# Moving matmul operands to chosen byte offsets within a partition: three unused tiles in a two-layer decoder trunk

## The chip, the cores and the metric

The kernel runs on one core of one Trainium2 chip. The metric is the device time of one execution in microseconds, as the median of several runs. Loading the inputs from the host is not in it; every weight is read from the chip's HBM within it.

## The reference

Two decoder layers over 256 tokens with a model width of 1024, in float32. Layer 0 mixes tokens with multi-head latent attention, layer 1 with MoBA block attention (at 256 tokens it is one causal block) and a shared relative bias. A dense MLP follows each.

```python
def sq_relu_mlp(h, w_in, w_out):          # (256,1024) @ (1024,4096), then @ (4096,1024)
    a = jax.nn.relu(h @ w_in)
    return (a * a) @ w_out

for i in range(2):
    h = rms_norm(x, attn_norm[i])
    x = x + (mla_mixer(h, ...) if i == 0 else moba_mixer(h, ...))
    h = rms_norm(x, mlp_norm[i])
    x = x + sq_relu_mlp(h, mlp_w_in[i], mlp_w_out[i])
```

## The kernel before

All activations are held transposed, the feature dimension over the 128 partitions. For precision, each operand of a large matmul is split into a high part (`fp32r`, a rounded float32) and a low part, the rest. One product is then three matmuls into the same PSUM tile: high by high, low weight by high, high weight by low. `mm3` issues them, and `mm` (L77) is the line of nearly every matmul.

The weights stream through `units`, each a 128 by 1024 tile (4096 bytes in a partition) or less. SP loads a unit into one of four `raw` tiles, ScalarE rounds it into a `wh` tile (`hi`, L141), VectorE subtracts to make `wl` (`lo`, L150). `wh` and `wl` are rings of seven tiles each. The helper `fill` puts these conversions between groups of matmuls; the order of all instructions is written out by hand.

What the matmuls read:

- `hT` is the pair `hTh`, `hTl`, the normalized input of a layer, 8 blocks of 256 columns (1024 bytes each). The first half of an MLP (`first`) streams a block of it against 128 columns of a weight unit: 8 blocks by 3 matmuls make 24 for one output of 256 columns, 16 such outputs for each of two rounds `r`.
- `a` is the pair of hidden activations of an MLP, 16 blocks of 256 columns, and lives in the MLP's own pool. The second half of a round streams its 16 blocks against weight columns: 48 matmuls for each of 8 outputs `d`, so 384 in a round.
- `aT` is the pair of attention outputs, 8 blocks of 256 columns, one per head, in the pool of a layer's heads. The output projection (`o` and `col` in `run_heads`) streams it: 24 matmuls for each of 8 outputs.
- In the projections of queries, keys and values the roles are exchanged: the weights stream (512 columns), and `hT`, `cqT` or `ckvT` is the stationary operand.

In these, each column block of a weight unit is 512 bytes and each block of an activation 1024, so all slices of one tile start at the same remainder to 512. The pools lie one after the other in each partition, in the order in which they are opened: `const`, `wraw`, `wsp`, `work`, `small`, then the pools of the layers. From the sizes of the tiles, the starts before are:

| tile | start, bytes | past a multiple of 512 |
|---|---|---|
| `hTh`, `hTl` (in `const`) | 30848, 39040 | 128 |
| `raw`, `wh`, `wl` (4096 bytes each) | from 47264, 63648, 92320 | 160 |
| `aT`, layer 0 | 211168, 219360 | 224 |
| `aT`, layer 1 | 202240, 210432 | 0 |
| `a`, both MLPs | 178688, 195072 | 0 |
| `cqT`, `ckvT` | 164576 and on | 224 |

Of the kernel before, what the change touches and what calls it, by code (L numbers as in the profile page):

```python
# [10 lines left out]
F32 = mybir.dt.float32  # L11
# [5 lines left out]
AX = mybir.AxisListType  # L17

P = 128
D = 1024  # L20
S = 256
NT = S // P
KD = D // P
H = 8
# [16 lines left out]

GAINS = [("attn0", KD), ("attn1", KD), ("mlp0", KD), ("mlp1", KD), ("qa", QR // P), ("kva", KVR // P),
         ("qn", 1), ("kn", 1), ("mq", 1), ("mk", 1), ("thr", 1)]
# [6 lines left out]
NR = 2  # L50
NPAIR = DFF // (2 * P * NR)
RAW = 4
# [4 lines left out]
def trunk(ctx: ExitStack, tc: tile.TileContext, A, out):  # L57
    nc = tc.nc
    ctx.enter_context(tc.manual_schedule())
    const = ctx.enter_context(tc.tile_pool(name="const", bufs=1))  # L60
# [5 lines left out]

    def ps():
        return psum.tile([P, 512], F32, name="ps", tag="ps")

    def t2(*shape):  # L70
        return work.tile([P, *shape], F32, name="t2", tag="t2")

    def f32(ap):
        return ap.bitcast(F32)

    def mm(o, a, b, start, stop):
        nc.tensor.matmul(o, a, b, start=start, stop=stop)  # L77

    def mm3(o, a, b, start, stop):

        mm(o, a[0], b[0], start, False)
        mm(o, a[1], b[0], False, False)
        mm(o, a[0], b[1], False, stop)
# [69 lines left out]
    def fill(n=1):  # L153
        lo(n)
        hi(n)

    def unit(i):
        while len(his) <= i:
            hi()
        while len(los) <= i:  # L160
            lo()
        return his[i], los[i]

    def done(i):

        used[0] = max(used[0], i + 1)

    def part(u, sl):
        return u[0][:, sl], u[1][:, sl]
# [9 lines left out]
    rowc = const.tile([P, HALF + 2 * PE_D], F32)  # L179
    xs = early.tile([P, NT, D], F32)  # L180
    warm = const.tile([P, 1], F32)
# [4 lines left out]
    nc.scalar.activation(warm, warm, AF.Sin)  # L186

    pz = ps()
    for _ in range(8):
        mm(pz, zeros[:, :P], zeros, True, True)  # L190
# [49 lines left out]

    hTh = const.tile([P, KD, S], F32R)
    hTl = const.tile([P, KD, S], F32R)

    def make_h(k, gname):

        nc.scalar.activation(hTh[:, k], x[:, k], AF.Copy, scale=gain(gname, k))
        nc.vector.scalar_tensor_tensor(hTl[:, k], x[:, k], gain(gname, k), f32(hTh[:, k]),
                                       op0=OP.mult, op1=OP.subtract)

    def hT(k, sl=slice(None)):  # L250
        return hTh[:, k, sl], hTl[:, k, sl]
# [33 lines left out]
    def row_scale(name, ss):  # L285

        m = small.tile([P, NT], F32, name="me_" + name, bufs=1)
        nc.vector.tensor_scalar(m, ss, 1.0 / D, EPS, op0=OP.mult, op1=OP.add)
        r = small.tile([P, NT], F32, name="rs_" + name, bufs=1)
# [44 lines left out]
    def to_T(y, dst, g):  # L334

        pt = ps()
        yf = y.rearrange("p a b -> p (a b)")
        for i in range(4):
            nc.tensor.transpose(pt[:, i * P:(i + 1) * P], yf[:, i * P:(i + 1) * P], ident)  # L339
        src = pt.rearrange("p (a b) -> p a b", b=P)  # L340
        if g is None:
            nc.scalar.copy(dst, src)
        else:
            nc.scalar.activation(dst, src, AF.Copy, scale=g)
# [52 lines left out]
    for k in range(KD):  # L397
# [6 lines left out]
        lo()  # L404
    LK = KVR + PE_D
    latq = [ps()[:, :QR] for _ in range(NT)]
    latk = [ps()[:, :LK] for _ in range(NT)]

# [37 lines left out]
    ssl = small.tile([P, 4, NT], F32, name="ssl", bufs=1)  # L446
    sqj = [early.tile([P, D], F32, name=f"sqj{i}") for i in range(2)]

# [36 lines left out]
    def head_tiles(l):  # L485

        cm = ExitStack()
        pool = cm.enter_context(tc.tile_pool(name=f"heads{l}", bufs=1))
        r = []
        for c in range(2):  # L490
            r.append({n: pool.tile([P, *sh], F32, name=f"{n}{c}")
                      for n, sh in (("k", (HG, S)), ("q", (HG, S)), ("v", (NT, HG, P)))})
        aT = [pool.tile([P, H, S], F32R, name=f"aT{i}") for i in range(2)]
        return cm, r, aT

# [260 lines left out]
    def mean_squares(i, n):  # L756
        nc.vector.scalar_tensor_tensor(msl[:, i], ssl[:, 1 + i], 1.0 / n, me0, op0=OP.mult, op1=OP.add)
        nc.vector.tensor_scalar(epsm[:, i], msl[:, i], EPS, None, op0=OP.mult)

    nc.vector.tensor_scalar(me0, ssl[:, 0], EPS / D, EPS * EPS, op0=OP.mult, op1=OP.add)  # L760
    mean_squares(0, KVR)
# [8 lines left out]
    lo()  # L770
    early_ctx.close()
    heads_ctx, hd, aT = head_tiles(0)
    mean_squares(2, QR)

# [14 lines left out]
    for o, a, b in rope_halves(m[:, :, 0], m[:, :, 1]):  # L789
        a, b = (i[:, :, None, :].to_broadcast([P, NT, 2, HALF]) for i in (a, b))  # L790
# [45 lines left out]
    def mlp(l, base, fillers, finish):  # L836

        with tc.tile_pool(name=f"mlp{l}", bufs=1) as pool:
            scale = pool.tile([P, S], F32, name="scale")
            a = [pool.tile([P, 2 * NPAIR, S], F32R, name=f"a{i}") for i in range(2)]  # L840
            sums = SumSquares()

            def first(b, r, j, split_k):
                u = [unit(b + 2 * j + i) for i in range(2)]
                if split_k:
                    o = [ps()[:, :S] for _ in range(2)]
                else:
                    p = ps()
                    o = [p[:, f * S:(f + 1) * S] for f in range(2)]
                for f, k in [(f, k) for k in range(KD) for f in range(2)] if split_k else \  # L850
                        [(f, k) for f in range(2) for k in range(KD)]:
                    c = (k % 4) * 256 + f * P
                    mm3(o[f], part(u[k // 4], slice(c, c + P)), hT(k), k == 0, k == KD - 1)
                fill(2)
                for g in fillers:
                    if g[0] == (r, j):
                        g[1]()
                for f, n in ((0, 1), (1, 1)) if split_k else ((0, 2),):
                    src = o[f] if split_k else p
                    rl = t2(n * S)  # L860
                    nc.scalar.activation(rl, src, AF.Relu)  # L861
                    sq = t2(n * S)
                    nc.vector.scalar_tensor_tensor(sq, src, 0.0, rl, op0=OP.max, op1=OP.mult)  # L863
                    ah, al = (i[:, 2 * j + f:2 * j + f + n].rearrange("p a b -> p (a b)") for i in a)
                    nc.scalar.copy(ah, sq)  # L865
                    nc.vector.tensor_sub(al, sq, f32(ah))  # L866
                done(b + 2 * j + 1)

            for r in range(NR):
                b = base + r * (2 * NPAIR + 2 * KD)  # L870
                for j in range(NPAIR):
                    first(b, r, j, r == 0 and j == 0)
                    if r == 0 and 1 <= j < 5:
                        sums.add(j - 1)
                    if r == 0 and j == 5:
                        s = sums.total()
                    if r == 0 and j == 6:
                        pb = ps()
                        mm(pb[:, :S], ones, s, True, True)
                        nc.vector.tensor_scalar(scale, pb[:, :S], 1.0 / D, EPS, op0=OP.mult, op1=OP.add)  # L880
                        nc.vector.reciprocal(scale, scale)
                b += 2 * NPAIR
                for d in range(KD):
                    o = ps()[:, :S]
                    for f in range(2 * NPAIR):
                        u = unit(b + 2 * d + f // 8)
                        c = (f % 8) * P
                        mm3(o, part(u, slice(c, c + P)), (a[0][:, f], a[1][:, f]), f == 0, f == 2 * NPAIR - 1)
                        if f == 7:
                            fill()  # L890
                            done(b + 2 * d)
                    fill()
                    for g in fillers:
                        if g[0] == (r, NPAIR + d):
                            g[1]()
                    y = t2(S)
                    nc.vector.tensor_tensor(y, o, scale, op=OP.mult)  # L897
                    if r < NR - 1:
                        nc.gpsimd.tensor_add(x[:, d], y, x[:, d])  # L899
                    else:  # L900
                        finish(d, y)
                    done(b + 2 * d + 1)
# [70 lines left out]


    heads_ctx, hd1, aT1 = head_tiles(1)
    order1 = {"k0": 0, "q0": 1, "v0": 2, "k1": 3, "v1": 4, "q1": 5}
    r3, sq3 = [None], [None]
# [138 lines left out]
```

## Time and profile before

| | us |
|---|---|
| median of 3 runs | 584.32 (583.97 to 585.66) |
| the profiled execution, whole time | 585.61 |
| its span, first to last instruction | 583.8 |
| TensorE (PE) busy | 572.6 |
| PE weight loads (PEld) busy | 546.3 |
| VectorE (DVE) busy | 406.8 |
| ScalarE (ACT) busy | 307.0 |
| GpSimd (POOL) busy | 114.0 |

Matmuls are pipelined: the duration of one is longer than the distance from its start to the next one's start. Where the text speaks of a pitch, it is that distance, the mean of many.

### The profile page before, as it was taken

The numbers are of one execution on the slowest core, as the hardware profiler recorded it, in microseconds if no ns is written. First come the engines' busy times: TensorE is split into PE (matmuls) and PEld (weight loads), VectorE is DVE, ScalarE is ACT, GpSimd is POOL, SyncE is SP. The second block draws the span as 40 slices with busy tenths as digits, with TensorE's granted clock in tenths as the row PEclk, the third lists the DMA queues.
The fourth block names the chain that finished last, engine by engine and source line by source line (L and its number), as shares of the span: only waits on it lengthen the run. The fifth ranks groups of instructions, "written<-read, shape, count | busy, mean of one in ns | idle before, by whom it ended". The sixth has DMA issues, their size and how long they took to land.

```text
span 583.8 us, 10767 instructions
## 1 busy us (share of the span) xinstructions
PE 572.6 (98%) x4346; PEld 546.3 (94%) x4346; DVE 406.8 (70%) x646; ACT 307.0 (53%) x492; POOL 114.0 (20%) x119
## 2 busy tenths in 40 slices
PE   8898999999999999999999999999999999999997
PEld 6877999999999999999988888999999999999997
DVE  5697877678899987786648456776778555666541
ACT  5688775665523355544545465756664333555420
POOL 5875100022132200024314100000231322000100
PEclk9899999999999999999999999999999999999999
DMA  7732535565645546475644554345466665465630
GB/s 285 280 92 73 182 111 161 174 189 173 216 146 170 184 154 217 161 234 184 209 152 134 194 177 138 116 145 180 144 186 207 186 185 179 151 207 173 225 120 28
DMA packets 29265, 99.54 MB, mean 171 GB/s; under 512 B 4032, under 2 KB 4672, under 8 KB 29216
## 3 DMA queue, kind: packets, MB, share of 16 engines
q1 hardware_dynamic: 28736, 97.92, 52.6%
q0 software_dynamic: 336, 0.92, 0.4%
q8 instruction: 34, 0.56, 0.4%
q14 instruction: 15, 0.12, 0.1%
q10 hardware_dynamic: 144, 0.02, 0.0%
HBM read 97.79 MB, written 1.05 MB: 169 GB/s over the span
## 4 chain that ended last, share of the span: by engine, by line
PE 92%; POOL 4%; DMA 1%; DVE 1%; issue 1%; ACT 1%; SPq 0%; POOLq 0%
PE ps L77 90%; POOL hrs L238 1%; PE ps L339 1%; PE ps L535 1%; DMA rowc<-in_rowc 1%; POOL pr L370 1%; POOL rr L371 1%; POOL t L730 0%; POOL kk L365 0%; POOL kk L364 0%; DVE cqT L461 0%; DVE wl L150 0%; POOL scl L238 0%; ACT wh L141 0%; POOL t L779 0%
## 5 line engine op out<-in xcount | busy, mean ns | idle before, releaser
L141 ACT CAST wh<-raw 128x1024 fp32r<-128x1024 f32 x177 | 183.1, 1046 | 111.7 <-DMA raw<-in_w_out_mlp 63.2
L150 DVE TENSOR_TENSOR wl<-raw,wh 128x1024 fp32r<-128x1024 f32 x177 | 228.1, 1319 | 8.5 <-ACT wh L141 8.2
L77 PE MATMUL ps<-a,wh 128*128 128x256 f32 x1024 | 186.8, 283 | 0.0
L77 PEld LDWEIGHTS ps<-a,wh 128*128 128x128 f32 x1024 | 158.2, 188 | 0.0
L77 PE MATMUL ps<-hTh,wh 128*128 128x256 f32 x512 | 144.6, 282 | 0.0
L77 PE MATMUL ps<-a,wl 128*128 128x256 f32 x512 | 143.8, 281 | 0.0
L77 PE MATMUL ps<-hTh,wl 128*128 128x256 f32 x512 | 143.8, 281 | 0.0
L77 PE MATMUL ps<-hTl,wh 128*128 128x256 f32 x512 | 143.8, 281 | 0.0
L77 PEld LDWEIGHTS ps<-a,wl 128*128 128x128 f32 x512 | 97.0, 190 | 0.0
L77 PEld LDWEIGHTS ps<-hTh,wl 128*128 128x128 f32 x512 | 96.5, 188 | 0.1
L77 PEld LDWEIGHTS ps<-hTh,wh 128*128 128x128 f32 x512 | 96.5, 188 | 0.1
L77 PEld LDWEIGHTS ps<-hTl,wh 128*128 128x128 f32 x512 | 96.5, 188 | 0.0
L77 PE MATMUL ps<-aT,wh 128*128 128x256 f32 x256 | 51.3, 290 | 0.0
L77 PE MATMUL ps<-wh,hTh 128*128 128x512 f32 (+2 forms) x128 | 47.0, 397 | 1.6 <-ACT wh L141 1.5
L77 PE MATMUL ps<-wh,hTl 128*128 128x512 f32 (+2 forms) x128 | 45.3, 382 | 0.0
L899 POOL TENSOR_TENSOR x<-t,x 128x256 f32<-128x256 f32 x16 | 26.4, 1650 | 96.2 <-DVE t L897 96.2
L77 PE MATMUL ps<-wl,hTh 128*128 128x512 f32 (+2 forms) x128 | 45.0, 380 | 0.0
L863 DVE SCALAR_TENSOR_TENSOR t<-ps,t 128x512 f32<-128x512 f32 (+1 forms) x34 | 22.4, 658 | 28.9 <-ACT t L861 28.9
L897 DVE TENSOR_TENSOR t<-ps,scale 128x256 f32<-128x256 f32 x32 | 13.5, 421 | 40.7 <-PE ps L77 40.7
L77 PEld LDWEIGHTS ps<-aT,wh 128*128 128x128 f32 x256 | 40.6, 188 | 0.2
L866 DVE TENSOR_TENSOR a<-t,a 128x512 fp32r<-128x512 f32 (+1 forms) x34 | 22.5, 662 | 22.5 <-ACT a L865 22.5
L238 POOL TENSOR_TENSOR hrs<-hss,mhalf 128x4 f32<-128x4 f32 (+1 forms) x18 | 25.0, 1400 | 64.1 <-DVE hss L314 48.8
(157 smaller groups left out, 650.5 us busy)
## 6 DMA issues: line engine op xcount, KB each, us to landing
raw<-in_w_in_mlp SPq DMA_DIRECT2D x64, 512.0 KB, 4.1
raw<-in_w_out_mlp SPq DMA_DIRECT2D x64, 512.0 KB, 4.3
raw<-in_w_qkv SPq DMA_DIRECT2D x24, 512.0 KB, 4.0
raw<-in_w_u SPq DMA_DIRECT2D x8, 512.0 KB, 6.1
win<-in_w_in SPq DMA_DIRECT2D x8, 352.0 KB, 5.6
raw<-in_w_o0a SPq DMA_DIRECT2D x4, 512.0 KB, 3.5
raw<-in_w_o0b SPq DMA_DIRECT2D x4, 512.0 KB, 3.5
raw<-in_w_o1a SPq DMA_DIRECT2D x4, 512.0 KB, 4.2
```

The source lines that it names most:

```text
L77: nc.tensor.matmul(o, a, b, start=start, stop=stop)
L141: (eng.copy if eng is nc.scalar else eng.tensor_copy)(his[i][:, :w], raws[i][:, :w])
L150: eng.tensor_sub(los[i][:, :w], raws[i][:, :w], f32(his[i][:, :w]))
L238: nc.gpsimd.tensor_tensor(dst, t, mhalf[:, :n].rearrange("p (a b) -> p a b", b=t.shape[-1]) if len(t.shape) == 3 else mhalf[:, :n], op=OP.pow)
L339: nc.tensor.transpose(pt[:, i * P:(i + 1) * P], yf[:, i * P:(i + 1) * P], ident)
L370: eng.tensor_scalar(pr, kk, c, None, op0=OP.mult)
L371: eng.tensor_sub(rr, src, pr)
L535: nc.tensor.transpose(pt[:, i * P:(i + 1) * P], self.p[:, i * P:(i + 1) * P], ident)
L863: nc.vector.scalar_tensor_tensor(sq, src, 0.0, rl, op0=OP.max, op1=OP.mult)
L866: nc.vector.tensor_sub(al, sq, f32(ah))
L897: nc.vector.tensor_tensor(y, o, scale, op=OP.mult)
L899: nc.gpsimd.tensor_add(x[:, d], y, x[:, d])
```

## The change

A helper `room` allocates a tile that no instruction reads or writes. It is called three times: 416 bytes in `const` behind `hTh` and `hTl`, 224 bytes in the MLP's pool ahead of `a`, and 224 bytes in the heads' pool of layer 1 ahead of `aT` (0, so none, in layer 0). No instruction is added, removed or moved; what follows a room in a partition starts later.

```diff
+ROOM = {"hT": 416, "aT0": 0, "aT1": 224, "a": 224}
...
+    def room(pool, name):
+        if ROOM[name]:
+            pool.tile([P, ROOM[name] // 4], F32, name="room_" + name)
...
     hTh = const.tile([P, KD, S], F32R)
     hTl = const.tile([P, KD, S], F32R)
+    room(const, "hT")
...
+        room(pool, f"aT{l}")
         aT = [pool.tile([P, H, S], F32R, name=f"aT{i}") for i in range(2)]
...
             scale = pool.tile([P, S], F32, name="scale")
+            room(pool, "a")
             a = [pool.tile([P, 2 * NPAIR, S], F32R, name=f"a{i}") for i in range(2)]
```

The starts past a multiple of 512 after it, by the same sums: `hT` 128 (unmoved), `raw`, `wh` and `wl` 160 + 416 = 576, so 64; `aT` of layer 0 224 + 416 = 640, so 128; `aT` of layer 1 and `a` 0 + 416 + 224 = 640, so 128; `cqT` and `ckvT` 128.

## Rows read from the trace of the kernel before

**Rows 1.** The page: busy time of each engine; granted clock in 40 slices.

```profile
PE 572.6 (98%) x4346; PEld 546.3 (94%) x4346; DVE 406.8 (70%) x646; ACT 307.0 (53%) x492; POOL 114.0 (20%) x119
...
PEclk9899999999999999999999999999999999999999
```

**Rows 2.** The page: the chain that ended last, by engine.

```profile
PE 92%; POOL 4%; DMA 1%; DVE 1%; issue 1%; ACT 1%; SPq 0%; POOLq 0%
```

**Rows 3.** Groups by shape, PE: xcount | busy us, mean ns | idle before.

```profile
L77 PE MATMUL ps<-a,wh 128*128 128x256 f32 x1024 | 186.8, 283 | 0.0
L77 PE MATMUL ps<-hTh,wh 128*128 128x256 f32 x512 | 144.6, 282 | 0.0
L77 PE MATMUL ps<-a,wl 128*128 128x256 f32 x512 | 143.8, 281 | 0.0
L77 PE MATMUL ps<-hTh,wl 128*128 128x256 f32 x512 | 143.8, 281 | 0.0
L77 PE MATMUL ps<-hTl,wh 128*128 128x256 f32 x512 | 143.8, 281 | 0.0
L77 PE MATMUL ps<-aT,wh 128*128 128x256 f32 x256 | 51.3, 290 | 0.0
L77 PE MATMUL ps<-wh,hTh 128*128 128x512 f32 x96 | 38.7, 403 | 0.0
...
L77 PE MATMUL ps<-aT,wl 128*128 128x256 f32 x128 | 35.8, 280 | 0.0
```

**Rows 4.** Timeline of PE, second MLP: start us, duration us, operation, xcount merged.

```profile
441.88 0.28 PE L77 MATMUL ps<-a,wh 128*128 128x256 f32 x1
...
487.95 0.28 PE L77 MATMUL ps<-hTh,wh 128*128 128x256 f32 x1
...
533.38 0.28 PE L77 MATMUL ps<-a,wh 128*128 128x256 f32 x1
```

**Rows 5.** Timeline of PE, output projection of layer 0: first and last.

```profile
87.70 0.28 PE L77 MATMUL ps<-aT,wl 128*128 128x256 f32 x1
...
100.19 0.28 PE L77 MATMUL ps<-aT,wh 128*128 128x256 f32 x1
```

**Rows 6.** Timeline of PE, output projection of layer 1: first and last.

```profile
383.17 0.28 PE L77 MATMUL ps<-aT,wl 128*128 128x256 f32 x1
...
395.89 0.28 PE L77 MATMUL ps<-aT,wh 128*128 128x256 f32 x1
```

**Rows 7.** Timeline of PE, projections of layer 1: first and last.

```profile
288.73 0.39 PE L77 MATMUL ps<-wh,hTh 128*128 128x512 f32 x1
...
305.29 0.39 PE L77 MATMUL ps<-wl,hTh 128*128 128x512 f32 x1
```

**Rows 8.** Timeline of PE, a query projection of layer 0: first and last.

```profile
33.02 1.56 PE L77 MATMUL ps<-wh,cqT 128*128 128x512 f32 x6
...
38.62 0.86 PE L77 MATMUL ps<-wl,cqT 128*128 128x512 f32 x3
```

**Rows 9.** Timeline of PE, two heads of layer 1, operands in full float32.

```profile
356.60 0.81 PE L77 MATMUL ps<-pT,v 128*128 128x256 f32 x4
357.25 0.82 PE L77 MATMUL ps<-k,q 128*128 128x128 f32 x4
```

**Rows 10.** Windows: us, busy (xcount) by engine, granted clock, DMA share, GB/s.

```profile
160.00:170.00 10.00, 10.00 (x90) 9.93 (x88) 9.76 (x14) 3.67 (x4) 3.31 (x2) 1.00 0.46 128
...
441.00:488.00 47.00, 47.00 (x394) 47.00 (x393) 28.21 (x27) 18.49 (x20) 11.53 (x7) 1.00 0.65 192
488.00:533.00 45.00, 45.00 (x382) 45.00 (x382) 28.83 (x31) 24.35 (x30) 1.65 (x1) 1.00 0.53 175
```

**Rows 11.** Waits from 396 us on: waiter <- releaser: us in total, times, longest.

```profile
ACT wh L141 <- DMA raw<-in_w_out_mlp: 36.9, 29, 3.6
```

## The prediction

> **What bounds the kernel now.** I read the page from the top. TensorE is busy for 98% of the span at nearly the full granted clock [rows 1], and the chain of work that ended last runs through it for 92% [rows 2]. The groups by shape show which matmuls these are: 1536 that stream `hT` (three groups of 512), 1536 that stream `a` (1024 and 512) and 384 that stream `aT` (256 and 128), all of 256 columns and with 0.0 us idle before them [rows 3]. The reader is to see that nothing ahead of TensorE holds it up in these groups; in the windows of the second MLP it is busy for 47.00 of 47 us and 45.00 of 45, at a granted clock of 1.00 [rows 10]. There the time is the number of matmuls times their pitch, and the only thing that the change can touch on this path is the pitch.
>
> The duration column is no pitch (283 ns for one matmul, while the next starts sooner), so I took pitches from the timeline, and found that they differ by tile although all are 128 by 256 with the same kind of weights:
>
> - `hT`: from 487.95 to 533.38 us stand one round's 16 outputs of 24, so 384 matmuls: 45.43 / 384 = 118.31 ns [rows 4].
> - `a`: from 441.88 to 487.95 us, 8 outputs of 48, again 384: 46.07 / 384 = 119.97 ns [rows 4].
> - `aT` in layer 0: 107 matmuls from 87.70 to 100.19 us: 12.49 / 106 = 117.83 ns [rows 5].
> - `aT` in layer 1: 107 matmuls from 383.17 to 395.89 us: 12.72 / 106 = 120.00 ns [rows 6].
>
> The last two are the telling pair. They come from the same lines of code in the same order, and one has the pitch of `a`, the other does not. What `aT` of layer 1 has in common with `a` is its start, 0 past a multiple of 512; `aT` of layer 0 starts at 224. The weights start at 160 in all four. So the pitch goes with where the operands start, by about 2 ns of 120, and the sum is made of such differences.
>
> **The change part by part.** It issues nothing, so there is no instruction to cost. It moves three things on the path: the weights from 160 to 64, `a` and `aT` of layer 1 from 0 to 128, `aT` of layer 0 from 224 to 128. `hT` stays at 128. In each large matmul of 256 columns the streamed tile then starts 64 bytes past the weights in the 512-byte grid.
>
> Before, only `aT` of layer 0 stands so (224 - 160 = 64), and it has the lowest pitch. `hT` is at 128 - 160 = -32 and `a` at -160. I take the distance between the two operands as what decides, so 117.83 ns for all, since it is the one row that shares something with every pair after the change. The terms:
>
> - `a`: 1536 x (119.97 - 117.83) = 3.29 us [rows 3 to 5].
> - `hT`: 1536 x (118.31 - 117.83) = 0.74 us [rows 3 to 5].
> - `aT` of layer 1: 192 x (120.00 - 117.83) = 0.42 us [rows 5, 6].
> - `aT` of layer 0: the distance stays, 0.
>
> That is 4.45 us. But the exact pair (128 with 64) is in no row, and the weights at a multiple of 64 are in none, so the price of a matmul is bounded from both sides. Below, by the wide matmuls: with `hT` stationary, 72 of 512 columns take 288.73 to 305.29 us, 16.56 / 71 = 233.24 ns, half of which is 116.62 ns for 256 columns [rows 7]. A matmul of twice the columns for each weight load has less room for a meeting of the two reads, so I take that as the pitch with none. Above, by the dearest row, 119.97. I choose 117.83 between them because the same distance gave it.
>
> The wide matmuls themselves have the weights as the streamed operand: distance 160 - 128 = 32 before, 64 - 128 = -64 after. With `cqT` stationary (start 224) it is -64 already before, and 24 of them from 33.02 to 38.62 us take 5.60 / 24 = 233.3 ns [rows 8], the same as at 32. So their term is 0.
>
> The engines that convert weights and activations get new addresses too; I cost that at nothing. In the second MLP VectorE is busy for 28.21 of 47 us and ScalarE for 18.49 [rows 10], and cover remains if their operations get a tenth longer. The tightest place is in the first MLP, where the bias blocks are made: VectorE is busy for 9.76 us of a window of 10 [rows 10]. If TensorE gets 1.8% faster there, VectorE needs 9.94 of 10. It still fits; if it did not, at most the gain of that half round is lost, 384 x 2.14 ns = 0.8 us. DMA moves at a share of 0.65 in the busier window [rows 10]; ScalarE waits for its loads, 36.9 us in the last third [rows 11], but its results are early, as TensorE shows no idle time there. A 2% faster consumer leaves that so.
>
> **Sum.** The profiled execution took 585.61 us, 1.81 us more than its span of 583.8, and stands 1.29 us above the median of 584.32. The saving lies inside the span, so I subtract it from the median: 584.32 - 4.45 = 579.9 us.
>
> **A rule that speaks against it.** By rows 5 and 6 the start of an operand goes with the pitch. The Trainium skill (SBUF — State Buffer, section "Who interferes with whom") gives TensorE two independent SBUF read ports, one for the moving operand and one for weight loads, and says that it never waits on anyone. By that rule the starts could not matter and the time would stay at 584.3 us. The rows show 117.83 against 120.00 ns, so I side with them, but keep the rule's outcome as a rival.
>
> **The rivals.**
>
> *The streamed tile's own start decides, not the distance.* `hT` lies at 128 already and shows 118.31 ns; after the change all of them lie there. Then `a` saves 1536 x 1.66 = 2.55 us, `aT` of layer 1 192 x 1.69 = 0.32, `aT` of layer 0 loses 192 x 0.48 = 0.09: 584.32 - 2.78 = 581.5 us. For it: `a` and `aT` of layer 1 share start and pitch. Against: the same two share the distance as well, so the rows can't tell.
>
> *No meeting is left.* All four go to 116.62 ns: 1536 x 1.69 + 1536 x 3.35 + 192 x 3.38 + 192 x 1.21 = 8.6 us, so 575.7. For it: the starts become multiples of 64 on both sides, which no pair before has. Against: nothing in the rows shows that this helps.
>
> *The base rate was held up too.* The full float32 matmuls run 768 columns (two heads, 256 + 128 each) in 0.65 us [rows 9], 0.846 ns a column. If the split ones could run at half of that, 0.423, 256 columns would take 108.3 ns; so 1536 x 10.0 + 1536 x 11.7 + 192 x 11.7 + 192 x 9.5 = 37.4 us, and with 288 wide ones (three groups of 96 [rows 3]) at 216.6, 288 x 16.6 = 4.8 us more: 542 us. Against: the wide matmuls show 0.456 ns a column at two different distances [rows 7, 8], so this base has not moved with the start.
>
> *Nothing changes.* The difference between the two `aT` comes from something else that differs between the layers, and the room does no more than shift addresses: 584.3. Against: the pitch of `a` repeats in `aT` of layer 1 within 0.03 ns.
>
> *Slower: weights at 64 meet the streamed tile worse.* The two tiles whose streamed start is a multiple of 64 (`hT`, `a`) have the higher pitches, the one whose start is not (`aT` of layer 0) the lowest. After the change all are multiples of 64, and the weights too. If that puts every pair at the level of `a`, `hT` loses 1536 x 1.66 = 2.55 us and `aT` of layer 0 192 x 2.14 = 0.41: 587.3 us. It decides from a mean pitch of about 119.1 ns on, the mean of `hT` and `a` now.
>
> **How the numbers follow.** The distance decides: 0.36 (579.9 us, its own range 578.5 to 581.2). The streamed start decides: 0.18. No meeting left: 0.20. Base rate: 0.04. Nothing: 0.10. Slower: 0.12. A measurement of this kernel can't tell less than about 0.3%, 1.75 us, from no change. The gains by distance, by start and by the lowest pitch lie beyond that; with a little of the second falling short, faster has 0.76, the same 0.12, slower 0.12. The range leaves out the base rate and the slower case (0.16): from 575.7 to 584.3, with the runs' own scatter of 0.9 us on both sides, 574.8 to 585.2.
>
> **What the profile after would show.** If the forecast holds: one round of `a` in the second MLP takes 384 x 117.8 = 45.2 us instead of 46.07, one of `hT` 45.2 instead of 45.43, `aT` of layer 1 falls to that of layer 0, and wide matmuls stay at 233 ns. If the streamed start decides, `a` falls to 118.3 and `hT` keeps its pitch, while `aT` of layer 0 rises. TensorE stays busy throughout and its granted clock at 1.00. The prediction is wrong if `hT`, whose tile does not move, changes by more than 1 ns, for then the weights' own start counts for more than the distance; or if gaps appear between the outputs in the first MLP, where VectorE has little room.

## The result

The changed kernel took 581.18 us (median of 6 runs, 580.05 to 581.82) against 584.15 for the kernel before (6 runs, 583.66 to 585.66): a ratio of 0.9938, 95% interval 0.9923 to 0.9952. The forecast was 579.9 us with a range of 574.8 to 585.2. Timed again on another occasion against 11 runs of before, it came out at 0.9911 (0.9896 to 0.9926). The forecast saving of 4.45 us, a ratio of 0.9924, lies at the edge of both intervals, which is where the first part of the execution comes in (below).

The page of the changed kernel, busy time and granted clock, answers to [rows 1]:

```profile
span 579.5 us, 10767 instructions
PE 567.9 (98%) x4346; PEld 541.0 (93%) x4346; DVE 406.6 (70%) x646; ACT 307.0 (53%) x492; POOL 115.8 (20%) x119
...
PEclk9998999999999999999999999999999999999999
```

The instructions are the same in number. TensorE's busy time fell by 4.7 us, that of its weight loads by 5.3 and the span by 4.3; POOL's rose by 1.8, and those of DVE and ACT hardly moved. The timeline of PE in the second MLP, at the same places as [rows 4]:

```profile
439.47 0.28 PE L84 MATMUL ps<-a,wh 128*128 128x256 f32 x1
...
484.70 0.28 PE L84 MATMUL ps<-hTh,wh 128*128 128x256 f32 x1
...
529.93 0.28 PE L84 MATMUL ps<-a,wh 128*128 128x256 f32 x1
```

Both rounds of 384 now take 45.23 us, 117.79 ns a matmul, where `a` took 46.07 and `hT` 45.43. The output projections of layer 0 and of layer 1, the first and the last of 107 matmuls each, answer to [rows 5, 6]:

```profile
87.68 0.28 PE L84 MATMUL ps<-aT,wl 128*128 128x256 f32 x1
...
100.16 0.28 PE L84 MATMUL ps<-aT,wh 128*128 128x256 f32 x1
...
381.21 0.28 PE L84 MATMUL ps<-aT,wl 128*128 128x256 f32 x1
...
393.70 0.28 PE L84 MATMUL ps<-aT,wh 128*128 128x256 f32 x1
```

12.48 / 106 = 117.7 ns and 12.49 / 106 = 117.8: layer 1 has come down from 120.0 to the pitch that layer 0 had all along. The wide matmuls, 72 from 286.74 to 303.30 us, take 16.56 / 71 = 233.2 ns, as in [rows 7].

**Where the saving sits.** The first matmul of the first MLP, in the timelines of before and after:

```profile
100.31 0.28 PE L77 MATMUL ps<-hTh,wh 128*128 128x256 f32 x1
...
100.28 0.28 PE L84 MATMUL ps<-hTh,wh 128*128 128x256 f32 x1
```

It starts at 100.31 us before and at 100.28 after, so nothing was gained ahead of it. From there to the end of the span it is 583.8 - 100.31 = 483.5 us before and 579.5 - 100.28 = 479.2 after: all of the 4.3 us. By stretches, 1.96 us of it lie between the start of the first MLP and the wide matmuls (188.42 to 186.46 us), 0.23 in the output projection of layer 1 (13.03 to 12.80) and 2.12 in the second MLP (183.34 to 181.22, first start to last).

**Why the medians differ less.** Windows of the changed kernel (us, busy and count by engine, granted clock, DMA share, GB/s):

```profile
30.00:45.00 15.00, 13.15 (x60) 9.88 (x59) 14.60 (x30) 11.77 (x34) 13.12 (x12) 1.00 0.31 89
45.00:50.00 5.00, 4.70 (x22) 3.78 (x21) 3.41 (x6) 2.92 (x12) 3.99 (x4) 0.66 0.30 108
```

The same kernel in another profiled execution:

```profile
10.00:15.00 5.00, 3.97 (x15) 3.97 (x16) 4.47 (x8) 4.54 (x9) 4.41 (x8) 0.66 1.04 405
...
45.00:50.00 5.00, 4.70 (x32) 3.88 (x31) 3.46 (x7) 4.29 (x17) 3.99 (x4) 1.00 0.34 108
```

In the first, the granted clock falls to its lower level (1.2 instead of 2.4 GHz) for part of the window from 45 to 50 us, after 15 us in which TensorE was busy for 13.15. In the second it falls earlier, between 10 and 15 us, and not again after 15 us with the same busy time; ten more matmuls fit into the last window, and the first MLP starts at 98.76 us instead of 100.28. The early fall was made up at once: from 20 to 25 us TensorE is busy for 4.43 us in the second execution and for 2.88 in the first. The profile of before has its fall between 20 and 30 us (0.83). So where the clock falls moved the start of the first MLP by some 1.5 us between two executions of one kernel. Behind it the second profile needs 577.9 - 98.76 = 479.1 us, like the first. It was the median of before that differed between the two occasions (584.15 and 585.51 us; the changed kernel had 581.18 and 581.16). A scatter of 1.5 us is large enough for that, but of before only one execution has a trace, so it is not shown that the clock was the cause there.

### The profile page after: what moved, and what is told of

Its sections match the earlier page's. It is cut to its first block, busy times and chain, and to the rows that moved or that the text cites. A ratio compares the mean times of both kernels' runs of the same rounds, so it can differ in the third digit from the quotient of the medians.

```text
span 579.5 us, 10767 instructions
## 1 busy us (share of the span) xinstructions
PE 567.9 (98%) x4346; PEld 541.0 (93%) x4346; DVE 406.6 (70%) x646; ACT 307.0 (53%) x492; POOL 115.8 (20%) x119
## 4 chain that ended last, share of the span: by engine, by line
PE 92%; POOL 4%; DVE 1%; DMA 1%; issue 1%; SPq 0%; ACT 0%; POOLq 0%
PE ps L84 90%; POOL hrs L245 1%; PE ps L347 1%; PE ps L544 1%; DMA rowc<-in_rowc 1%; POOL pr L378 1%; POOL rr L379 1%; POOL t L739 0%; POOL kk L373 0%; POOL kk L372 0%; DVE sqj L462 0%; DVE cqT L469 0%; DVE wl L157 0%; POOL scl L245 0%; POOL rr L383 0%
## 5 line engine op out<-in xcount | busy, mean ns | idle before, releaser
L84 PE MATMUL ps<-a,wh 128*128 128x256 f32 x1024 | 183.5, 280 | 0.0
L84 PEld LDWEIGHTS ps<-a,wl 128*128 128x128 f32 x512 | 95.8, 187 | 0.0
```

## The experiments

All but the first have the change's `room` helper and one more call ahead of `hTh`, so that any start can be set; the edits are given against the changed kernel. "Distance" is the start of the streamed tile less that of the weights. Pitches are worked out from the timeline, over a round of 384 matmuls of the second MLP for `hT` and `a`, over 106 intervals for `aT`. Experiments 3 to 7, 9 and 10 are one execution each (584.75, 583.47, 585.68, 581.14, 584.77, 574.07 and 580.69 us), so their pitches and stretches are read and not their times.

**1. The changed kernel once more** (no edit).

> The changed kernel itself, unchanged, timed in five rounds. Its traced span fell by 4.3 us against that of before (583.8 to 579.5), while the medians fell by 2.97 (584.15 to 581.18). If the pitch is the whole effect and the rest is where in the first 50 us the granted clock drops, the difference of the medians comes out between 3.0 and 4.5 us here. If the change costs something outside the matmuls of the sum, it stays at 3.0 or below.

Measured: 581.16 us (579.73 to 581.22) against 585.51: 0.9911 (0.9896 to 0.9926), a difference of 4.35 us, within the 3.0 to 4.5 expected. No cost outside the matmuls shows.

**2. The same distance at other starts.**

```diff
-ROOM = {"hT": 416, "aT0": 0, "aT1": 224, "a": 224}
+ROOM = {"hT0": 96, "hT": 416, "aT0": 0, "aT1": 224, "a": 224}
```

> All starts 96 bytes further: weights at 160 past a multiple of 512 (as before the change), hT, a and aT at 224, so the distance is 64 in every pair and no start is a multiple of 64. If the distance decides, every pitch is 117.8 ns as in the changed kernel and the time is the same as its, about 581. If starts at multiples of 64 or the weights' own start decide, the pitches of hT and a go back to between 118.3 and 120.0 ns and the time to 582.5 to 584.3.

The timeline of PE, starts of the rounds:

```profile
438.32 0.28 PE L84 MATMUL ps<-a,wh 128*128 128x256 f32 x1
...
483.55 0.28 PE L84 MATMUL ps<-hTh,wh 128*128 128x256 f32 x1
...
528.77 0.28 PE L84 MATMUL ps<-a,wh 128*128 128x256 f32 x1
```

45.23 and 45.22 us, 117.8 ns each: at this distance the pitch stays when every start moves by 96 bytes, and multiples of 64 have no part in it. The time is 580.47 us (0.9906, 0.9882 to 0.993), that of the changed kernel within the intervals.

**3 and 4. One part of the change alone.** First only the room behind `hT` (weights and all behind them move), then only the rooms ahead of `a` and `aT` of layer 1.

```diff
+ROOM = {"hT0": 0, "hT": 416, "aT0": 0, "aT1": 0, "a": 0}      # onlyW
+ROOM = {"hT0": 0, "hT": 0, "aT0": 0, "aT1": 224, "a": 224}    # onlyA
```

> The room behind hT alone: weights at 64, hT at 128, a and aT of layer 1 at 416 (distance 352, which is 96 by 256), aT of layer 0 at 128. If the distance to 256 bytes decides: hT 117.78 ns, a and aT of layer 1 stay at 119.97 although they moved by 416 bytes, and the span is 0.8 us below that of before for the same first 100 us. If the weights' own start decides, a falls to 117.78 too.

> The rooms ahead of a and of aT of layer 1 alone: weights stay at 160, a and both aT at 224 (distance 64), hT at 128 (distance -32). If the distance decides: a and aT 117.78 ns, hT stays at 118.31; 3.4 us less from a and 0.4 us from aT. If multiples of 64 are what helps, a does not fall.

The starts of the rounds with the weights alone moved, then with `a` and `aT` alone moved:

```profile
441.23 0.28 PE L84 MATMUL ps<-a,wh 128*128 128x256 f32 x1
...
487.31 0.28 PE L84 MATMUL ps<-hTh,wh 128*128 128x256 f32 x1
...
532.53 0.28 PE L84 MATMUL ps<-a,wh 128*128 128x256 f32 x1
```

```profile
441.44 0.28 PE L84 MATMUL ps<-a,wh 128*128 128x256 f32 x1
...
486.67 0.28 PE L84 MATMUL ps<-hTh,wh 128*128 128x256 f32 x1
...
532.10 0.28 PE L84 MATMUL ps<-a,wh 128*128 128x256 f32 x1
```

With the weights alone moved, a round of `hT` takes 532.53 - 487.31 = 45.22 us (117.8 ns, though `hT` itself has not moved) and one of `a` 487.31 - 441.23 = 46.08 (120.0 ns, though `a` has moved by 416 bytes). With `a` alone moved it is the other way round: `a` 486.67 - 441.44 = 45.23, `hT` 532.10 - 486.67 = 45.43. Counted from the first matmul of the first MLP to the end, the first part saves 483.5 - (582.9 - 100.17) = 0.8 us and the second 483.5 - (581.6 - 101.79) = 3.7. Together 4.5, where the whole change saves 4.3: the parts add up.

**5 and 6. Other distances**, weights at 64 throughout.

```diff
+ROOM = {"hT0": 32, "hT": 384, "aT0": 448, "aT1": 480, "a": 384}    # sweepA
+ROOM = {"hT0": 480, "hT": 448, "aT0": 128, "aT1": 320, "a": 288}   # sweepB
```

> Weights at 64, four distances in one kernel: hT at 96 bytes past the weights, a at 224, aT of layer 0 at 0, aT of layer 1 at 320. If the distance decides and repeats every 256 bytes: hT 119.97 ns (as -160 before), a 118.31 (as -32 before), aT of layer 1 117.78 (as 64). If it repeats only every 512, these three are unknown between 116.6 and 120. If only the weights' own start (64) decides, all are 117.78. Distance 0 is in no row so far: 116.6 if equal starts never meet, 120 or more if they always do.

> Weights at 64, four more distances: hT at 32, a at 128, aT of layer 1 at 160, aT of layer 0 at 192. If the distance decides, each has its own pitch between 116.6 ns (half of a wide matmul) and about 120; if only the weights' own start decides, all are 117.78. A distance with less than 117.5 ns would point to a faster version.

The first of these kernels, starts of the rounds of `a` and `hT`:

```profile
442.59 0.28 PE L84 MATMUL ps<-a,wh 128*128 128x256 f32 x1
...
488.03 0.28 PE L84 MATMUL ps<-hTh,wh 128*128 128x256 f32 x1
...
534.10 0.28 PE L84 MATMUL ps<-a,wh 128*128 128x256 f32 x1
```

45.44 us (118.3 ns at 224) and 46.07 us (120.0 ns at 96): the pitches that -32 and -160 had before, to 0.05 ns. `aT` of layer 1 at 320 has that of 64. So at the three distances tried twice, 64, 96 and 224, the pitch repeats after 256 bytes. The second kernel, first and last of 107 matmuls of `aT` in layer 0, then the rounds:

```profile
87.67 0.28 PE L84 MATMUL ps<-aT,wl 128*128 128x256 f32 x1
...
99.69 0.28 PE L84 MATMUL ps<-aT,wh 128*128 128x256 f32 x1
...
439.07 0.28 PE L84 MATMUL ps<-a,wh 128*128 128x256 f32 x1
...
484.63 0.28 PE L84 MATMUL ps<-hTh,wh 128*128 128x256 f32 x1
...
529.44 0.28 PE L84 MATMUL ps<-a,wh 128*128 128x256 f32 x1
```

12.02 / 106 = 113.4 ns at distance 192, lower than anything else and lower than half of a wide matmul. Collected, by distance to 256 bytes (0, 32, 128 and 160 with one tile only):

| distance | 0 | 32 | 64 | 96 | 128 | 160 | 192 | 224 |
|---|---|---|---|---|---|---|---|---|
| pitch, ns | 120.0 | 116.7 | 117.8 | 120.0 | 118.6 | 117.3 | 113.4 | 118.3 |

That of 128 holds for the second MLP; a stretch of 191 in the first (263.94 to 286.73 us) took 22.79 / 190 = 119.9. It was the first sign that a distance need not have one pitch only.

**7. Finer steps around 192.** Each tile is made 256 bytes longer and used from an offset on, as here for `hT`; the same for `a` (176), `aT` of layer 0 (184) and of layer 1 (200).

```diff
+ROOM = {"hT0": 128, "hT": 288, "aT0": 96, "aT1": 96, "a": 64}
...
-    hTh = const.tile([P, KD, S], F32R)
-    hTl = const.tile([P, KD, S], F32R)
+    hTh, hTl = (const.tile([P, KD * S + 64], F32R, name=n)[:, 4:4 + KD * S].rearrange("p (a b) -> p a b", b=S)
+                for n in ("hTh", "hTl"))
```

> Steps finer than 32 bytes around distance 192, weights at 64: hT at 208, a at 176, aT of layer 0 at 184, aT of layer 1 at 200. If the pitch runs smoothly with the distance, 184 and 200 stay near 113 to 114 ns and 176 and 208 between 113.4 and the neighbours at 160 and 224 (117.3 and 118.3). If it goes in steps of 32 bytes (or of 64), 200 and 208 have the pitch of 192 (113.4) and 176 and 184 that of 160 (117.3).

Neither. `hT` at 208 takes 532.84 - 487.08 = 45.76 us, 119.2 ns; `a` at 176 takes 45.79, 119.2; `aT` at 184 and at 200 takes 12.71 and 12.73 us for 106, 119.9 and 120.1. None of the four odd distances is as good as any multiple of 32 but 0 and 96. The gain at 192 is a point, not a slope. In this kernel the streamed tiles' own starts are no multiples of 32 either, while the weights stay at 64; whether that or the distance makes these four slow is not separated.

**8. Distance 192 for all.**

```diff
+ROOM = {"hT0": 128, "hT": 288, "aT0": 128, "aT1": 96, "a": 96}
```

> Weights at 64, hT, a and both aT at distance 192 (start 0 or 256 past a multiple of 512). The aT of layer 0 took 113.44 ns at that distance. If the pitch is a function of the distance to 256 bytes alone, all 3456 matmuls of 256 columns take 113.4 ns, and the time falls by 3456 x 4.34 = 15.0 us below the changed kernel's, to about 566. If 113.44 belonged to something else about aT of layer 0, hT and a stay at 116.7 ns or above and the time at 577 or above.

572.23 us (569.14 to 575.33), a ratio of 0.9786 (0.9753 to 0.9819): faster than the changed kernel, but short of 566, and with a spread of 6 us. The timeline of PE, layer 1's MLP:

```profile
386.26 0.28 PE L84 MATMUL ps<-hTh,wh 128*128 128x256 f32 x1
...
424.23 0.28 PE L84 MATMUL ps<-hTl,wh 128*128 128x256 f32 x1
424.35 0.59 PE L84 MATMUL ps<-ssum,ones 128*128 128x256 f32 x2
424.59 0.47 PE L84 MATMUL ps<-hTh,wh 128*128 128x256 f32 x1
...
430.43 0.28 PE L84 MATMUL ps<-a,wh 128*128 128x256 f32 x1
...
475.65 0.28 PE L84 MATMUL ps<-hTh,wh 128*128 128x256 f32 x1
...
520.88 0.28 PE L84 MATMUL ps<-a,wh 128*128 128x256 f32 x1
```

The first 336 matmuls of `hT` take 37.97 / 335 = 113.3 ns. Then two matmuls for the norm come between, and from there on the rounds take 45.22 and 45.23 us, 117.8 ns, at the same addresses. The distance of 192 has two pitches. Three rounds, 1152 matmuls, at the higher one are 1152 x 4.5 = 5.2 us of the 15.0 that were expected.

**9. The same kernel, profiled again.**

> The kernel with distance 192 everywhere, once more, for a second profile. Its first profile shows two pitches, 113.4 and 117.8 ns, at one distance, each kept for as long as no gap came between the matmuls. If a start after a gap falls into one of two modes by chance, the same stretches now show other pitches in places: the three long rounds of the second MLP, 117.78 in the first profile, may be at 113.4, and the span lies anywhere from about 568 to 574. If the mode belongs to the place in the program, every stretch repeats its pitch.

The same places:

```profile
388.08 0.28 PE L84 MATMUL ps<-hTh,wh 128*128 128x256 f32 x1
...
432.25 0.28 PE L84 MATMUL ps<-a,wh 128*128 128x256 f32 x1
...
477.47 0.28 PE L84 MATMUL ps<-hTh,wh 128*128 128x256 f32 x1
...
522.70 0.28 PE L84 MATMUL ps<-a,wh 128*128 128x256 f32 x1
```

45.22 and 45.23 us again, and 113.3 ns until 426.05 us. In these two profiles the pitch goes with the place in the program: every long stretch repeats it. The short stretches of the first MLP behind 156 us, some at 113.3 and some at 117.8 ns, repeat theirs too, in these two profiles and in those of experiments 11 and 12, which leave that part alone.

The beginning of `a` in the first MLP does not repeat. In the first profile:

```profile
142.14 0.28 PE L84 MATMUL ps<-a,wh 128*128 128x256 f32 x1
...
147.33 0.44 PE L84 MATMUL ps<-a,wh 128*128 128x256 f32 x2
147.60 0.28 PE L84 MATMUL ps<-a,wl 128*128 128x256 f32 x1
...
153.16 0.28 PE L84 MATMUL ps<-a,wh 128*128 128x256 f32 x1
```

The 45 matmuls up to 147.33 us have the higher pitch. The next one (the second of the line of two) starts some 0.15 us later instead of 0.118, with no other matmul between, and from 147.60 us on 50 matmuls take 5.56 us / 49 = 113.5 ns. In the second profile the same happens at a step of 0.14 us at 139.74, still in `hT`, and in that of experiment 12 at one of 0.25 us at 148.79. In that of experiment 11 no step of these 96 matmuls is late, and all keep the higher pitch. So one matmul that starts late is enough to change the pitch, here from the higher to the lower; what makes it late, these lines do not show.

Nor does the place settle it for executions without a trace. Those of experiment 8 run from 569.14 to 575.33 us, and the fastest, with the same granted clock (1.0) as the profiled one of 572.29, is 3.1 us shorter. That other stretches were at the lower pitch there is likely, but not shown.

**10. Low parts of the weights 64 bytes further.** An unused tile of 64 bytes between the two weight rings; the rooms ahead of `a` and `aT` are 64 bytes smaller.

```diff
+                if i == 0:
+                    wsp.tile([P, 16], F32, name="room_wl", tag="room_wl", bufs=1)
                 los.append(wsp.tile([P, 1024], F32R, name="wl", tag="wl"))
```

> As the kernel with distance 192 everywhere, but the low parts of the weights 64 bytes further, so hT, a and aT are 192 past wh and 128 past wl. In mm3 the order is high weight, low weight, high weight. If a stream is held up by the load of the next weights, the first of the three (streams while the low weights are loaded) pays; if by a meeting with its own weights, the second pays. With the single prices, the mean is (118.6 + 2 x 113.4) / 3 = 115.2 ns; 113.4 if the low weights don't matter.

Inconclusive as to which of the three pays: the rounds take 45.40 and 45.39 us, 118.2 ns, more than the 115.2 of the expectation. That sum took the lower pitch of 192; with the higher one the single prices give (118.6 + 2 x 117.8) / 3 = 118.1, so the run does not speak against adding them. The low weights do count: 118.2 ns is neither pitch of 192, and the first 336 matmuls of `hT`, at 113.3 ns with distance 192 alone, have it too (392.52 to 432.13 us, 39.61 / 335).

**11. A small matmul behind every 48 of the second MLP**, at distance 192 (behind each output of `a` and each pair of outputs of `hT`, 32 in all).

```diff
+                if l == 1:
+                    mm(ps()[:, :2], zeros[:, :P], zeros[:, :2], True, True)
                 fill(2)
...
+                    if l == 1:
+                        mm(ps()[:, :2], zeros[:, :P], zeros[:, :2], True, True)
                     fill()
```

> The kernel with distance 192 everywhere and, in the second MLP alone, one more matmul of 2 columns behind every output (32 in all, at most 0.1 us each, so up to 3 us). If a gap lets the mode be drawn anew, the second MLP shows both pitches, changing only at these places, and the spread between executions (569.1 to 575.3) gets narrower round a mean of about 115.6 ns for it. If the mode is set otherwise, the long rounds keep one pitch and the time is just longer by the added matmuls.

The timeline of PE round one of them:

```profile
393.58 0.28 PE L84 MATMUL ps<-hTl,wh 128*128 128x256 f32 x1
393.70 0.18 PE L84 MATMUL ps<-zeros 128*128 128x2 bf16 x1
393.74 0.36 PE L84 MATMUL ps<-hTh,wh 128*128 128x256 f32 x1
393.94 0.28 PE L84 MATMUL ps<-hTh,wl 128*128 128x256 f32 x1
```

Not both pitches but the low one after every added matmul, between 113.3 and 113.7 ns. A group of 48 now starts 399.52 - 393.94 = 5.58 us after the one before (second matmul to second matmul), 0.14 more than 48 at 113.3 ns, so the 32 cost some 4.5 us; expected were 0.1 us each and up to 3 us. At the pitch of 117.8 a group takes 5.65. The time was 573.55 us (573.17 to 574.74): the second MLP needs 571.6 - 388.25 = 183.4 us, 0.8 less than with distance 192 alone, the low pitch gained and nearly all of it paid for the gaps. The spread between executions did get narrower.

**12. Two of them, where the pitch is lost.**

```diff
+                if l == 1 and r == 0 and j >= 6:
+                    mm(ps()[:, :2], zeros[:, :P], zeros[:, :2], True, True)
                 fill(2)
```

> The kernel with distance 192 everywhere and only two added matmuls of 2 columns, in the second MLP behind outputs 6 and 7 of the first round of hT (the gap behind output 6 is where both profiles of the kernel with distance 192 fall from 113.3 to 117.8 ns and then keep it to the end). If the place of a start, with what came just before it, sets the mode, as the kernel with 32 added matmuls showed, the remaining some 1200 matmuls run at 113.4 to 113.7 ns: 1200 x 4.2 = 5.0 us less and 0.5 us for the two gaps, so about 567.5 where distance 192 alone gave 572.2. If the low pitch was only kept because every output had a gap, the long rounds fall back to 117.78 and the time stays at 572 or above.

```profile
426.13 0.18 PE L84 MATMUL ps<-zeros 128*128 128x2 bf16 x1
426.17 0.68 PE L84 MATMUL ps<-ssum,ones 128*128 128x256 f32 x2
...
432.14 0.18 PE L84 MATMUL ps<-zeros 128*128 128x2 bf16 x1
432.18 0.36 PE L84 MATMUL ps<-a,wh 128*128 128x256 f32 x1
...
475.80 0.28 PE L84 MATMUL ps<-hTh,wh 128*128 128x256 f32 x1
...
519.32 0.28 PE L84 MATMUL ps<-a,wh 128*128 128x256 f32 x1
```

The round of `hT` takes 519.32 - 475.80 = 43.52 us, 113.3 ns, and those of `a` keep that pitch too. The second MLP, from its first matmul (388.04 us) to the end of the span (567.2), takes 179.2 us, against 570.4 - 386.26 = 184.1 with distance 192 alone: 4.9 us (expected were 5.0 less and 0.5 for the gaps, 4.5 in all). The median is 570.02 us (568.79 to 573.17), a ratio of 0.9747 (0.9718 to 0.9776), the lowest of all. Its interval overlaps that of distance 192 alone, so it is the stretch in the trace, not the medians, that shows the 4.9 us, in one traced execution here against two at distance 192 alone. Behind the first of the two added matmuls stand the norm's own two, and the pitch stays low across them. 567.5 was not reached in the median; the profiled execution took 568.98.

## Why the prediction was right, and where it was off

- *The distance between the streamed tile and the weights decides.* Right, and shown: by experiment 2 (other starts, same distance, same pitch), by `hT`, which fell from 118.31 to 117.79 ns without being moved (less than the 1 ns that was to refute the forecast), and by 3 and 4, in which each tile follows the distance and not its own start. The rival by the streamed start and the slower one by multiples of 64 both fall with experiment 2; "no meeting is left" asked for 116.62 ns and "nothing changes" for 119.97 in `a`, where 117.79 was measured. By the ports' rule of the Trainium skill (SBUF — State Buffer, "Who interferes with whom") all pitches of the table would be one. The runs show 113.4 to 120.0 ns, and the measurement decides.
- *One distance, one pitch* was taken for granted, and that it came out was in part luck. At 64 it held, 117.8 ns in every long stretch; at 128 and 192 it does not, and no row of before could tell which kind 64 is.
- *The terms.* By the pitches after, `a` saves 1536 x (119.97 - 117.79) = 3.35 us against 3.29 and `hT` 0.80 against 0.74; wide matmuls 0 against 0. For `aT` of layer 1 the pitch came as forecast, but of its 0.42 us the trace has 0.23: 108 of the 192 matmuls stand in the output projection, and the other 84, among the heads, saved nothing (from the first wide matmul to the output projection it is 94.24 us before and 94.27 after). The trace has 4.3 us behind the first 100.
- *The time.* 581.18 against 579.9 us. I took the saving that one trace gives off the median of three runs; the first 100 us, which gained nothing, differ by 1.5 us between two profiles of the changed kernel. On the other occasion the difference was 4.35.
- *Cover.* VectorE was busy for 9.84 us of the window from 160 to 170 (9.76 before, [rows 10]), and the stretches of `a` there run at 117.8 ns as well. The tightest place held.
- *The lower bound* was wrong. I took half of a wide matmul, 116.62 ns, as the pitch with no meeting of the two reads. At distance 192 it is 113.4, and the wide ones moved as well: with `hT` 192 bytes past the weights, 72 of them take 280.90 to 297.15 us, 16.25 / 71 = 228.9 ns instead of 233.2. A row that does not change between two distances is no base. The forecast did not hang on it, but the rival "no meeting is left" had its price from there, and a better version would have been missed.

What stays open: why the pitch has these values at these distances, why 192 has two, and how a gap or a late matmul picks one of them. That two reads meet in the memory is a picture that fits, and no run shows it.

## What to carry to other kernels

Where TensorE is the bound and the same matmul shape shows different pitches for different tiles, compare the tiles' byte offsets before anything else: here a few hundred bytes of unused room were worth 0.6 to 0.9%, and the best distance found 2.1%. One profile tells several distances if each operand is given its own, so a whole table costs two more runs. Take the pitch from starts in the timeline, over long unbroken stretches, and look at every stretch: a mean would have hidden that one distance has two.

## What the runs showed of the hardware

- The pitch of 128 by 256 `fp32r` matmuls runs from 113.3 to 120.1 ns with the distance of the two operands' starts, repeats after 256 bytes at the distances tried twice, and was worse (119.2 to 120.1 ns) at the four distances tried that are no multiple of 32.
- At distance 192 there are two lasting pitches, 113.3 and 117.8 ns, the higher of which is also the one pitch seen at distance 64. Rounds of 384 keep either to the end. A gap can change it (113.3 to 117.8 behind the norm's matmuls), and so can one matmul that starts 0.02 to 0.13 us late with no other between (117.8 to 113.3).
- With a 2-column matmul ahead of a stream the lower pitch stood in all 33 places tried, two of them with the norm's matmuls between; in each the stream before it was at the lower one too, so that such a matmul can switch from the higher is not shown.
- The granted clock fell to its lower level for a few us within the first 50 in every profile but the first of distance 192, at different places (0.66 from 10 to 15 us, 0.83 from 20 to 30, 0.66 from 45 to 50). Between two profiles of the changed kernel that moved everything behind it by some 1.5 us.
